# Conditioning weights' blocks begin four panels later in the queue of weight transfers of a flow-matching block

## The chip, the cores and the metric

One core of a Trainium2 chip runs the kernel. The metric is device time in microseconds (us), the median of several executions. Besides these, one execution was profiled; all rows shown here come from it, and their times count from the start of its span.

## What is computed

One layer of a hybrid backbone, float32 throughout: 256 latent tokens and 256 context tokens of width 1024.

```python
sh1, sc1, g1, sh2, sc2, g2 = split(silu(c) @ w_ada + b_ada, 6)     # w_ada: 1024 x 6144
z = modulate(layer_norm_plain(x), sh1, sc1) @ w_in + b_in          # w_in: 1024 x 5904
# p -> pooling mixer, (q, k, v, gates, o) -> mLSTM, (u, v) -> spatial gating, mg -> merge gates
y = (sig(mg_p)*(pool @ w_bp) + sig(mg_m)*(mlstm @ w_bm) + sig(mg_s)*(sgu @ w_bs)) @ w_out
x = layer_norm(alpha*x + g1*y, ln1_g, ln1_b)
h = modulate(layer_norm_plain(x), sh2, sc2)
f = top-4-of-32 clamped SwiGLU experts(h)                          # 12 MB of weights each
out = layer_norm(alpha*x + g2*f, ln2_g, ln2_b)
```

The first third of `w_ada` (`sh1`, `sc1`) is wanted before the input projection. The other two thirds (`g1`, `sh2` and `sc2`, `g2`) are wanted only behind the merge: these are the conditioning weights of the title, 16 blocks of 128 x 2048 floats (1 MB each), called `("ada", 1, k)` and `("ada", 2, k)`, k from 0 to 7.

## The kernel before

**Transfers.** All weights come through one hand-written list, `queue`, issued on SyncE (SP) by `pump` (L149) in list order. A block goes to a free 1 MB slot of the SBUF arena; there are six slots until the merge (an expert's blocks take two slots each). `done(key)` (L174) frees a slot and pumps, so the instruction that last reads a block releases the transfer that comes next in the list; SP works its issues off in order.

**Panels.** `w_in` is cut into 23 blocks `("win", i)` of 256 columns, "panels". A panel is split in two rounded parts so that three matmuls make a float32 product: `split` (L340) casts it on ScalarE (L343), and `low`, run later by `tick`, subtracts on VectorE (L348) and frees its slot. The matmuls of a projection are L251.

**Order of the front part.** The code writes every engine's instructions in one order:

- the first two panels (key columns), then value columns (`v_unit`), each with a piece of convolution (L441, L443) on VectorE;
- a loop over four query units (L991 to L1002); between them steps of `gates` (mLSTM gates; PE L502 to L546, VectorE L510 to L559);
- a loop over 17 `panels` (L1052), each with two units of 24 matmuls. In order: 8, 9, 10, 6, 7, then 11 to 22 (merge gates); below they are "panel loop 0 to 16". Between units, `next(side)` advances a generator `chain` (L957): `state` (VectorE L578, PE L577 and L586, ScalarE L580, L588), `sgu` (PE L743, VectorE L746), `pooling`, `heads` (PE L604 to L628, ScalarE L613, VectorE L615, L633), `head_out`;
- the merge (L1079), the output projection, normalization and routing, and the 32 experts (L1484).

PSUM banks are handed round in small rings: `sps()` has two banks for `gates`, `state`, `sgu` and `heads`.

**Conditioning steps.** `ada_step` (L392) stands at the end of every unit. It takes one conditioning block if that block is the oldest loaded block not yet used: a panel that was loaded before it and is not yet freed blocks it. The first block of each group is scaled on ScalarE (`S.mul`, L398), the seven others are one VectorE instruction over 2048 columns that adds the block before, which is then freed:

```python
V.scalar_tensor_tensor(out=w, in0=w, scalar=sc_[:, k:k + 1], in1=weight(("ada", g, k - 1)), op0=ALU.mult, op1=ALU.add)
done(("ada", g, k - 1))
```

After the last block of a group `ada_reduce` (L407) sums over partitions on TensorE (L417 or L422, L427).

Of the kernel before, what the change touches and what calls it, by code (L numbers as in the profile page):

```python
# [117 lines left out]
def kernel(ctx, tc, x, cx, cols, rows, csts, wsm, wgt, bada, brt, sgub, bdn, bgu,  # L118
# [11 lines left out]
    late = [(("ada", g, k), wada[P * k:P * k + P, 2048 * g:2048 * g + 2048]) for g in (1, 2) for k in range(KB)]  # L130
# [2 lines left out]
    queue.insert(5, (("win", 1), win[1]))  # L133
    for n, i in enumerate([2, 3, 4, 5, 8, 9, 10, 6, 7] + list(range(11, 23))):
        queue.append((("win", i), win[i]))
        if 2 <= n < 18:
            queue.append(late.pop(0))
    queue += [(("br", i), wbr[i]) for i in range(4)]
    queue += [(("out", i), wout[i]) for i in range(4)]
    for e in range(NE):  # L140
# [1548 lines left out]
```

## Time and profile before

| | us |
|---|---|
| median of 3 executions (1279.19 to 1282.16) | 1281.83 |
| the profiled execution, device time | 1278.06 |
| its span | 1276.3 |
| TensorE (PE) busy | 1184.0 (93%) |
| VectorE (DVE) busy | 462.5 (36%) |
| ScalarE (ACT) busy | 285.2 (22%) |

The mean granted clock of TensorE was 0.989. The span holds two very different parts: up to about 320 us the front part, then the experts. So shares of the span say little, and the rows below are of single stretches.

### The profile page before, as it was taken

To read this page: it belongs to the slowest core of one execution; us is meant where nothing else is said; L and a number is where in the kernel's file an instruction comes from. 1 tells how busy PE (TensorE), PEld (TensorE's weight loads), DVE (VectorE), ACT (ScalarE), POOL (GpSimd) and SP (SyncE) were. 2 spreads that over 40 slices of the span, in tenths; PEclk is the share of its full clock that TensorE was granted. 3 is DMA by queue.
4 is the path that set the end of the run, shared out by engine and by line. 5 is a ranking of instruction groups with operands and counts; after the bars stand their busy time and mean duration, and the time that the engine had idled before them with its cause. 6 is when DMAs were issued, how large, how long until landed. Compare 5 with 4: busy or idle time off the path is not lost. (4 is left out here: it accounts for less than half of the span.)

```text
span 1276.3 us, 16505 instructions
## 1 busy us (share of the span) xinstructions
PE 1184.0 (93%) x6619; PEld 609.9 (48%) x6624; DVE 462.5 (36%) x988; ACT 285.2 (22%) x548; POOL 28.4 (2%) x42
## 2 busy tenths in 40 slices
PE   7997999998999999999999999999898998889885
PEld 5897889996333334334433333333333333333321
DVE  6478758796322222222212222222222122222223
ACT  5352655734111111111111111111111111111101
POOL 1000000102000000000000000000000000000000
PEclk9998999998999999999999999999999999999998
DMA  9745657778899999999969999999999999999994
GB/s 390 270 151 215 218 194 284 293 306 322 354 425 426 426 426 427 426 379 428 375 238 386 428 426 427 426 425 427 427 427 426 425 426 427 427 426 425 428 422 179
DMA packets 39758, 471.74 MB, mean 370 GB/s; under 512 B 4561, under 2 KB 4689, under 8 KB 7761
## 3 DMA queue, kind: packets, MB, share of 16 engines
q1 hardware_dynamic: 37440, 464.01, 87.9%
q10 hardware_dynamic: 1552, 4.14, 1.0%
q8 instruction: 89, 1.46, 0.5%
q0 software_dynamic: 640, 1.84, 0.4%
q14 instruction: 37, 0.30, 0.1%
HBM read 468.92 MB, written 1.05 MB: 368 GB/s over the span
## 5 line engine op out<-in xcount | busy, mean ns | idle before, releaser
L1397 PE MATMUL bank<-arena,arena 128*64 128x512 f32 x1808 | 408.9, 596 | 18.1 <-DMA arena<-in_wgu_dram 17.5
L1419 PE MATMUL bank<-arena,arena 128*64 128x512 f32 x1088 | 248.3, 597 | 25.1 <-DMA arena<-in_wdn_dram 17.8
L1397 PEld LDWEIGHTS bank<-arena,arena 128*64 128x64 f32 x1808 | 124.0, 137 | 259.8 <-issue 235.2
L1419 PEld LDWEIGHTS bank<-arena,arena 128*64 128x64 f32 x1088 | 78.6, 136 | 171.9 <-issue 148.9
L251 PE MATMUL bank<-rounded 128*128 128x256 f32 (+1 forms) x1152 | 149.5, 289 | 0.1
L251 PEld LDWEIGHTS bank<-rounded 128*128 128x128 f32 x1152 | 143.9, 195 | 1.8 <-issue 0.6
L1402 DVE TENSOR_SCALAR arena<-bank 128x256 f32<-128x256 f32 x68 | 28.9, 425 | 279.1 <-PE bank L1397 279.1
L1422 DVE SCALAR_TENSOR_TENSOR arena<-bank,arena,g2q 128x512 f32<-128x512 f32 x33 | 24.8, 751 | 266.7 <-PE bank L1419 147.0
L1403 ACT ACTIVATE arena<-arena 128x256 f32<-128x256 f32 x68 | 28.5, 419 | 364.5 <-DVE arena L1402 360.6
L1412 ACT COPY arena<-bank 128x256 f32<-128x256 f32 x68 | 25.4, 373 | 290.5 <-PE bank L1411 290.5
L1397 PE MATMUL bank<-arena 128*64 128x512 f32 x368 | 83.7, 597 | 3.7 <-DMA arena<-in_wgu_dram 3.4
L348 DVE TENSOR_TENSOR rounded<-arena,rounded 128x2048 fp32r<-128x2048 f32 x29 | 66.3, 2285 | 15.1 <-ACT rounded L343 15.1
L1372 PE MATMUL bank<-arena 128*128 128x128 f32 (+1 forms) x576 | 69.9, 275 | 0.0
L1372 PEld LDWEIGHTS bank<-arena 128*128 128x128 f32 x576 | 66.9, 192 | 0.8 <-DVE arena L1404 0.7
L1375 ACT ACTIVATE arena<-bank,shc 128x128 f32<-128x128 f32 (+1 forms) x144 | 53.4, 452 | 51.4 <-PE bank L1372 51.4
L343 ACT CAST rounded<-arena 128x2048 fp32r<-128x2048 f32 x29 | 55.1, 1899 | 11.4 <-PE bank L251 5.6
L1384 DVE TENSOR_SCALAR rounded<-bank 128x256 fp32r<-128x256 f32 x34 | 14.5, 425 | 116.1 <-PE bank L1383 116.1
L1397 PEld LDWEIGHTS bank<-arena 128*64 128x64 f32 x368 | 24.9, 137 | 53.3 <-issue 44.3
L1423 ACT CAST rounded<-arena 128x512 fp32r<-128x512 f32 x33 | 20.4, 619 | 109.4 <-DVE arena L1422 109.4
L1431 PE MATMUL bank<-rounded 64*128 64x512 f32 x264 | 40.7, 418 | 3.6 <-ACT rounded L1423 3.1
L1431 PEld LDWEIGHTS bank<-rounded 64*128 64x128 f32 x264 | 22.8, 184 | 33.9 <-issue 25.1
L1391 PE MATMUL bank<-rounded 128*128 128x512 f32 x68 | 32.4, 476 | 5.8 <-PEq L1508 3.7
(326 smaller groups left out, 890.3 us busy)
## 6 DMA issues: line engine op xcount, KB each, us to landing
arena<-in_wgu_dram SPq DMA_DIRECT2D x127, 2048.0 KB, 29.6
arena<-in_wdn_dram SPq DMA_DIRECT2D x62, 2048.0 KB, 28.0
arena<-in_win_dram SPq DMA_DIRECT2D x23, 1024.0 KB, 5.1
arena<-in_wada_dram SPq DMA_DIRECT2D x16, 1024.0 KB, 5.0
arena<-in_wad_dram SPq DMA_DIRECT2D x8, 1024.0 KB, 10.8
arena<-in_wbr_dram SPq DMA_DIRECT2D x4, 1024.0 KB, 5.6
arena<-in_wout_dram SPq DMA_DIRECT2D x4, 1024.0 KB, 5.6
arena<-in_wdn_dram SPq DMA_DIRECT2D x3, 1024.0 KB, 29.4
```

Source lines behind the costliest of these rows:

```text
L251: mm(o, l, r, start=start and n == 0, stop=stop and n == len(todo) - 1)
L343: S.copy(out=wh[:, 0:2048], in_=w)
L348: V.tensor_tensor(out=wl[:, 0:2048], in0=w, in1=wh[:, 0:2048].bitcast(F32), op=ALU.subtract)
L1372: mm(pg[:, w * k:w * k + w], h2[:, t, 512 * a + P * k:512 * a + P * k + P], b["sl"][:, t].rearrange("p i n -> p (i n)"), start=t == 0, sto ...
L1375: S.activation(out=b["hT"][:, 4 * a + k].rearrange("p i n -> p (i n)"), in_=pg[:, w * k:w * k + w], func=AF.Identity, scale=shc[:, 1, 4 * ...
L1391: mm(pg[:], bse[e % 2][:], bst[:, hf, :], start=True, stop=False, skip_group_check=True)
L1397: mm(pg[64 * q:64 * q + 64, :], hT[:, k, :], wk[:, k % 2, 512 * q:512 * q + 512], start=False, stop=k == KB - 1, skip_group_check=True)
L1402: V.tensor_scalar_min(gc[:], pg[:, 0:256], LIMIT)
L1403: S.activation(out=sg[:], in_=gc[:], func=AF.Sigmoid, scale=SW_ALPHA)
L1412: S.copy(out=b["gT"][:, 4 * hf:4 * hf + 4, :].rearrange("p (q j) n -> p j q n", q=2), in_=pt[:, 0:256].rearrange("p (j q n) -> p j q n", j ...
L1419: mm(py[64 * q:64 * q + 64, :], b["gT"][:, k, :], wk[:, k % 2, 512 * q:512 * q + 512], start=k == 0, stop=k == KB - 1)
L1431: mm(acc[t][hf][:], b["sT"][sl, P * t:P * t + P], y_[sl, :], start=False, stop=last and y_ is ylx, skip_group_check=True)
```

## The change

In the list, the 16 conditioning blocks stood one behind each of the panels number 2 to 17 (n counts panels from panel 2 on). Now the first stands behind n = 6, and n = 7, 9, 11 and 13 have two behind them; the last stands where it stood, behind n = 17. Nothing else is edited; which `ada_step` finds work follows from the list.

```diff
     for n, i in enumerate([2, 3, 4, 5, 8, 9, 10, 6, 7] + list(range(11, 23))):
         queue.append((("win", i), win[i]))
-        if 2 <= n < 18:
+        for _ in range(0 if n < 6 or n > 17 else 2 if n in (7, 9, 11, 13) else 1):
             queue.append(late.pop(0))
+    assert not late
```

## Rows read from the trace of the kernel before

**Rows 1.** Busy time by stretch: span, PE, PEld, DVE, ACT, POOL, granted clock, DMA share, GB/s.
```profile
100.00:125.00 25.00, 18.97 (x136) 17.09 (x137) 22.47 (x42) 4.90 (x8) 0.00 (x0) 0.91 0.56 200
...
150.00:175.00 25.00, 25.00 (x171) 20.95 (x171) 15.87 (x25) 14.87 (x27) 0.00 (x0) 1.00 0.59 210
175.00:200.00 25.00, 24.83 (x194) 22.89 (x190) 16.61 (x21) 13.18 (x25) 0.58 (x1) 1.00 0.62 215
...
325.00:350.00 25.00, 24.54 (x124) 9.73 (x122) 6.65 (x17) 3.71 (x9) 0.00 (x0) 1.00 1.00 415
```

**Rows 2.** Timeline of PE, 60 to 160 us: start, length, instruction, idle before.
```profile
97.02 1.23 PE L520 MATMUL bank<-ident,W 128*8 128x128 f32 x5 [2.37 <-DVE W L514]
97.90 4.19 PE L251 MATMUL bank<-rounded 128*128 128x256 f32 x24
...
116.17 0.44 PE L577 MATMUL bank<-ident,arena 128*128 128x128 f32 x2 [1.69 <-DVE Rc L553]
...
122.63 2.06 PE L586 MATMUL bank<-arena 128*128 128x258 f32 x4 [4.28 <-DVE arena L578]
124.13 4.78 PE L251 MATMUL bank<-rounded 128*128 128x256 f32 x24
...
128.96 1.04 PE L586 MATMUL bank<-arena 128*128 128x258 f32 x4
129.65 3.21 PE L251 MATMUL bank<-rounded 128*128 128x256 f32 x24
```

**Rows 3.** Timeline of DVE, the same stretch.
```profile
93.69 2.35 DVE L400 SCALAR_TENSOR_TENSOR arena<-arena,sc__144 128x2048 f32<-128x2048 f32 x1
95.95 0.48 DVE L455 TENSOR_SCALAR arena<-bank,col 128x256 f32<-128x256 f32 x1
...
98.58 2.35 DVE L400 SCALAR_TENSOR_TENSOR arena<-arena,sc__144 128x2048 f32<-128x2048 f32 x1
...
110.16 2.35 DVE L400 SCALAR_TENSOR_TENSOR arena<-arena,sc__144 128x2048 f32<-128x2048 f32 x1
...
119.14 2.35 DVE L400 SCALAR_TENSOR_TENSOR arena<-arena,sc__144 128x2048 f32<-128x2048 f32 x1
...
122.07 0.75 DVE L578 TENSOR_TENSOR arena<-arena,ee 128x258 f32<-128x258 f32 x2
```

**Rows 4.** Short stretches, columns as in the first group: where the clock was low.
```profile
96.00:100.00 4.00, 2.98 (x15) 2.65 (x16) 3.90 (x11) 0.44 (x2) 0.00 (x0) 0.61 0.92 346
...
124.00:128.00 4.00, 4.00 (x20) 3.85 (x19) 1.01 (x1) 2.17 (x2) 0.00 (x0) 0.55 0.47 197
```

**Rows 5.** Instructions of L400 and of L398: count, ns min/median/max, first and last start.
```profile
L400 DVE SCALAR_TENSOR_TENSOR arena<-arena,sc__144 x14: 2319/2345/2347, 93.7 to 221.8; 128x2048 f32<-128x2048 f32 x14
...
L398 ACT ACTIVATE arena<-arena,sc__144 x2: 2004/2010/2015, 79.7 to 158.8; 128x2048 f32<-128x2048 f32 x2
```

**Rows 6.** Timeline of all engines, 176 to 184 us (panel loop 7).
```profile
177.18 1.90 ACT L343 CAST rounded<-arena 128x2048 fp32r<-128x2048 f32 x1
...
179.12 2.29 DVE L348 TENSOR_TENSOR rounded<-arena,rounded 128x2048 fp32r<-128x2048 f32 x1 [1.36 <-ACT rounded L343]
...
181.32 0.42 DVE L746 TENSOR_TENSOR mx<-bank,arena 128x256 f32<-128x256 f32 x1
...
181.79 0.18 PEld L610 LDWEIGHTS bank<-rounded 40*128 40x128 f32 x1 [0.26 <-DVE mx L746]
```

**Rows 7.** Timeline of ACT from 158 us on.
```profile
205.01 1.90 ACT L343 CAST rounded<-arena 128x2048 fp32r<-128x2048 f32 x1
```

**Rows 8.** Timeline of DVE from 158 us on.
```profile
196.67 0.43 DVE L633 TENSOR_TENSOR arena<-bank,ni 128x258 f32<-128x258 f32 x1 [1.28 <-ACT ni L631]
198.46 2.29 DVE L348 TENSOR_TENSOR rounded<-arena,rounded 128x2048 fp32r<-128x2048 f32 x1 [1.36 <-ACT rounded L343]
```

**Rows 9.** DMA issues of the page: count, KB each, median us to landing.
```profile
arena<-in_win_dram SPq DMA_DIRECT2D x23, 1024.0 KB, 5.1
```

**Rows 10.** What SP waited for, 240 to 330 us: us in total, times, longest.
```profile
SPq L166 <- DVE rounded L348: 31.7, 4, 11.2
SPq L166 <- PEq L1508: 12.2, 1, 12.2
```

## The prediction

> **What bounds the kernel now.** I read the busy time by stretch first, then timelines of the engines where that view shows holes. The reader is to see two regimes. From 325 us on the DMA engines are full: a share of 1.00 and 415 GB/s, with PE at 24.54 of 25 us [rows 1]. That part, the experts, needs a fixed amount of data; it ends earlier only if it starts earlier. Before it, SP's waits are for releases of slots by L348 and the experts' own L1508 [rows 10], not for bandwidth: expert blocks are fetched when the front part sets space free, so what the front part gains, the end should gain.
>
> In the front part PE is full where the panel loop runs (25.00 and 24.83 of 25 us at 150 to 200), but between 100 and 125 us it is busy only 18.97, and there DVE is the full engine, 22.47 [rows 1]. The timeline of PE names the holes: 2.37 us for L514, 1.69 for L553, 4.28 for L578, each a short mixer instruction on DVE [rows 2]. The timeline of DVE shows why these are late: DVE runs almost without a pause, and conditioning steps of 2.35 us stand between its short instructions at 93.69, 98.58, 110.16 and 119.14 [rows 3]. Nothing wants their result before the merge.
>
> **Which steps move.** By the rule of `ada_step` I wrote down, unit by unit, which six blocks are loaded. Before, steps (1,1) to (1,3) fall in the query loop, (1,4) in panel loop 0, one each in 2, 3, 4, the ACT step (2,0) in 5, and one each in 6 to 12; the ACT step (1,0) falls between the value units at 79.7 [rows 5]. After, the list is 2, 3, 4, 5, 8, 9, 10, then (1,0), 6, (1,1), (1,2), 7, (1,3), 11 and so on. Panels now stand in front of the conditioning blocks, so no step finds work until panel 10 is freed: the ACT step (1,0) falls in panel loop 0, (1,1) and (1,2) in loop 2, (1,3) in 3, (1,4) and (1,5) in 4, (1,6) in 5, (1,7) and the ACT step (2,0) in 6, (2,1) in 7, (2,2) and (2,3) in 8. From loop 9 on both lists give the same step in the same unit. So four DVE steps leave 93 to 122 us, and loops 2 to 8 hold ten instead of six. The reduction of group 1 moves from loop 5 to loop 7 with the same matmuls. Bytes, instructions and transfers stay the same in number.
>
> **What leaves.** A step holds DVE for 2.26 us, from its start to that of the next instruction (93.69 to 95.95) [rows 3]. The first hole ends 2.26 us earlier, so 0.1 of 2.37 stays. L553 comes three steps (6.8 us) earlier, and the 1.69 goes. L578 comes four steps, 9.0 us, earlier: its end moves from 122.82 to 113.8. PE, without its holes, is there at 122.63 - 8.34 = 114.3, or about 113.2 with the full clock. The ACT step (1,0) now stands on ACT just ahead of the copy that L586 also needs, 2.0 us [rows 5], which puts that copy at about 114.0: I leave 0.8 of the third hole. Holes: 2.37 + 1.69 + 4.28 - 0.1 - 0.8 = 7.4 us.
>
> **The clock.** Behind the first and the third hole the granted clock is 0.61 and 0.55 over four us, stretches at the half level (1.2 GHz) [rows 4]. There 24 matmuls of L251 take 4.19 and 4.78 us where the same group takes 3.21 later, and L586 takes 2.06 where it later takes 1.04 [rows 2]: 1.0 + 1.6 + 1.0 = 3.6 us. With holes of 0.1 and 0.8 us I expect the clock to stay up and take all of it; the lower bound is nothing.
> The Trainium skill ("TensorE: Matmul & The Clock Gate", Part 1: The HAM clock gate) says that the full clock is held by activity, and that the moment of the change does not hang on the kernel's start, so the same kernel shows differing numbers of slow matmuls from run to run. The trace agrees that low clock follows holes (0.61 and 0.55); that it varies between executions no run here shows. By that rule these 3.6 us would come back only in some executions.
>
> **What arrives.** Loops 2 to 8 get four more DVE steps. DVE is busy 15.87 and 16.61 of 25 us there [rows 1]; over the 75 us of these loops 4 x 2.26 = 9.0 us more is about 3 in 25, which leaves DVE room. What counts is what is queued behind a step. In loops 2 to 5 it is mostly the next panel's L348, whose panel PE wants a loop later, or operands that `heads` wants one or two units later: nothing. One place is tight. In loop 7 the second L610 wants a bank of the two-bank ring that L746 must first empty; it already waits 0.26 us. L746 stands behind L348, and that waited 1.36 us for the cast at 177.18 [rows 6]. The moved ACT step (2,0) now stands directly in front of that cast: cast, L348, L746 and L610 come 2.0 us later. Lower bound zero, if ACT is early there; upper bound 2.0 [rows 5]. I take 2.0, because the chain has no slack in it now.
>
> In loop 8 the second step comes after L633 at 196.67 and ends some 2.4 us later, near 199.5; L348, now at 198.46, moves by 1.0 us [rows 8]. Its result is used in the last third of a unit that starts some 3 us later: nothing. That step also releases panel 18's transfer near 199.5 instead of one unit earlier; with 5.1 us to landing [rows 9] it is there at 204.6, against the cast at 205.01 [rows 7]. Hidden, with 0.4 us to spare; if it lands late, the cast waits, and the panel is used two loops later, so still nothing. All other panels arrive a loop or more ahead.
>
> **Sum.** -7.4 - 3.6 + 2.0 = -9.0 us. Against the profiled execution: 1278.06 - 9.0 = 1269.1. That execution is 3.8 us below the median of the three runs, and a new median will lie as those do: 1281.83 - 9.0 = 1272.8. I predict 1272.5.
>
> **Rivals.** A change under 0.3% (3.8 us) is about what a measurement of this kernel can't tell from none.
>
> *The clock doesn't come back.* The holes close, but PE still falls to half speed near the third hole, where 0.8 us of waiting stays beside short matmuls: -7.4 + 2.0 = -5.4, 1276.4. For it: the low clock lasts beyond the hole itself [rows 4]. Against it: later in the front part holes of some tenths leave it at 1.00 [rows 1].
>
> *The panel loops pay it back.* Steps are now doubled between mixer instructions whose PE partners follow a unit later; if three of the ten come through to PE, 3 x 2.26 = 6.8 goes: -2.2, 1279.6, within the 0.3%. For it: the tight ring in loop 7 [rows 6] shows that the margins of `heads` and `sgu` are short. Against it: ten steps where six cost PE almost nothing now (24.83 to 25.00 busy) [rows 1].
>
> *Hidden anyway.* If the experts' start hung on bandwidth, nothing would move: 1281.8. Against it: SP's waits for releases [rows 10].
>
> *Slower.* One mechanism: DVE's order in loops 2 to 8 becomes the bound, that is, every L348 and mixer instruction queues behind a step and PE waits out each. Ten steps then cost 22.6 us and the ACT step 2.0, against 11.0 gained: +13.6, 1295. It decides for slower once seven or more steps are exposed in full (7 x 2.26 = 15.8 with the ACT step's 2.0, less 11.0 and the 0.3%). For it: DVE is strictly in program order. Against it: a load of about 19 in 25 us, and PE without holes there now.
>
> **How the numbers follow.** Forecast (-6.5 to -12, so 1270 to 1275) 0.56; clock stays low 0.16; paid back 0.16; hidden 0.05; slower 0.07. Faster by over 0.3%: the first two and a little of the third, 0.74; same 0.19; slower 0.07. The range: its low end is the profiled execution less all of the gain without the 2.0, 1278.06 - 11.0 = 1267; its high end takes in the clock's case and most of the paid-back one, 1279.5.
>
> **What would show it.** In the changed profile: no L400 before about 115 us, and the first ten of the DVE steps between there and 200; PE without the three holes and DVE no longer at 22 in 25 at 100 to 125 us; granted clock 1.00 there; the first PE L586 near 114; a new wait of L610 for L746 in loop 7, some 2 us; the experts' first L1397, now at 315, about 9 us earlier, and the end by the same. Wrong would be: holes that stay at the same instructions with another releaser (ACT's copy for L586, the cast of panel 10), new holes at L610, L624 or L714 of the panel loop, or an expert part that starts earlier and ends no earlier.

## The result, and the profile after

The changed kernel took 1273.66 us (median of 7 runs, 1268.46 to 1275.1) against 1280.42 us (7 runs, 1278.16 to 1282.16) for the kernel before, run beside it: a ratio of 0.9941, 95% interval 0.9923 to 0.9959. It is faster by 0.6%. The forecast was 1272.5 us in a range of 1267 to 1279.5, with 0.74 on faster. The profiled execution took 1274.13 us, its span 1272.3 us at a mean granted clock of 0.990; before, these were 1278.06, 1276.3 and 0.989. In the changed kernel all lines from the list of transfers on are one higher: L251 is L252, L400 is L401, L586 is L587, L746 is L747.

First the busy time by stretch, in the columns of [rows 1], of the changed kernel.

```profile
100.00:125.00 25.00, 23.58 (x182) 21.86 (x181) 21.03 (x40) 12.32 (x17) 0.00 (x0) 1.00 0.41 136
125.00:150.00 25.00, 24.66 (x184) 21.01 (x183) 22.14 (x30) 17.51 (x32) 1.76 (x3) 1.00 0.87 301
150.00:175.00 25.00, 22.94 (x158) 19.87 (x157) 16.83 (x23) 13.17 (x25) 0.58 (x1) 0.93 0.62 217
175.00:200.00 25.00, 25.00 (x198) 23.88 (x197) 17.88 (x14) 11.89 (x16) 0.00 (x0) 1.00 0.75 262
```

TensorE went from 18.97 to 23.58 us busy between 100 and 125 us, and the clock from 0.91 to 1.00 [rows 1]. But the stretch from 150 to 175, full before at 25.00 us and 1.00, now stands at 22.94 us and 0.93: something new costs there. VectorE carries at 125 to 150 us what left the stretch before: 22.14 of 25 us, with TensorE at 24.66 beside it. In the kernel before it had 16.64 there:

```profile
125.00:150.00 25.00, 24.58 (x187) 22.69 (x188) 16.64 (x21) 15.68 (x26) 1.77 (x3) 0.95 0.55 199
```

The timeline of TensorE of the changed kernel, where [rows 2] showed the three holes:

```profile
94.82 0.71 PE L521 MATMUL bank<-ident,W 128*8 128x128 f32 x5
95.28 3.12 PE L252 MATMUL bank<-rounded 128*128 128x256 f32 x24
...
110.63 0.38 PE L578 MATMUL bank<-ident,arena 128*128 128x128 f32 x2
...
114.17 1.14 PE L587 MATMUL bank<-arena 128*128 128x258 f32 x4 [1.42 <-ACT arena L581]
114.96 3.23 PE L252 MATMUL bank<-rounded 128*128 128x256 f32 x24
118.02 0.38 PE L578 MATMUL bank<-ident,arena 128*128 128x128 f32 x2
118.25 1.04 PE L587 MATMUL bank<-arena 128*128 128x258 f32 x4
```

L521 and the second L578 follow the work ahead of them without a wait, where L520 had waited 2.37 us and L577 1.69 [rows 2]. L587 still waits 1.42 us in place of 4.28, and for another engine: ScalarE's copy L581. The group of 24 matmuls behind the first hole takes 3.12 us in place of 4.19, that behind the third 3.23 in place of 4.78. The second L587 starts at 118.25, where L586 started at 128.96: 10.7 us earlier.

Then the timelines of ScalarE and VectorE of the changed kernel around that wait:

```profile
111.72 0.24 ACT L561 ACTIVATE ee<-ee 128x48 f32<-128x48 f32 x1
111.87 1.99 ACT L399 ACTIVATE arena<-arena,sc__144 128x2048 f32<-128x2048 f32 x1
113.77 0.62 ACT L581 COPY arena<-bank 128x256 f32<-128x256 f32 x2
```

```profile
113.32 0.75 DVE L579 TENSOR_TENSOR arena<-arena,ee 128x258 f32<-128x258 f32 x2
...
120.50 2.35 DVE L401 SCALAR_TENSOR_TENSOR arena<-arena,sc__144 128x2048 f32<-128x2048 f32 x1
```

The scaling L399 stands directly ahead of L581. The first blending step L401 (one of the DVE conditioning steps) starts at 120.50, behind the products L579 for which the first two L587 wait; four such steps ran before 122 us in [rows 3]. L579 is 8.75 us earlier than L578 was.

Last, panel loop 7 of the changed kernel, in the timelines of ScalarE, VectorE and TensorE. In [rows 6] the second weight load L610 waited 0.26 us here.

```profile
162.96 2.00 ACT L399 ACTIVATE arena<-arena,sc__144 128x2048 f32<-128x2048 f32 x1
164.85 1.89 ACT L344 CAST rounded<-arena 128x2048 fp32r<-128x2048 f32 x1
```

```profile
166.78 2.29 DVE L349 TENSOR_TENSOR rounded<-arena,rounded 128x2048 fp32r<-128x2048 f32 x1 [3.25 <-ACT rounded L344]
168.99 0.42 DVE L747 TENSOR_TENSOR mx<-bank,arena 128x256 f32<-128x256 f32 x1
```

```profile
169.46 0.44 PE L611 MATMUL bank<-rounded 40*128 40x384 f32 x1 [1.90 <-DVE mx L747]
...
170.99 1.23 PE L629 MATMUL bank<-arena 128*128 128x258 f32 x2 [0.16 <-ACT arena L615]
171.66 4.34 PE L252 MATMUL bank<-rounded 128*128 128x256 f32 x24
```

The chain reads from top to bottom: scaling, cast, low part, L747, and TensorE waits 1.90 us. Behind the wait L629 takes 1.23 us and the 24 matmuls 4.34, where such groups take 0.70 and 3.23 at the full clock: 1.6 us more, at a granted clock of 0.73 from 172 to 176 us.

**Where the gain stands along the span.** In the two profiled executions, TensorE is ahead by 10.7 us at the second L587. Loop 7 takes 1.9 in the wait and 1.6 at half clock, of which 0.26 us of waiting was there before. In loop 9 the lead is 7.4 us and stays so until the gathers L1373, matmuls that pick the first experts' tokens once the routing is known. These take 5.44 us in place of 3.81, at a clock of 0.59 from 304 to 308 us. The kernel before has half clock in this stage too (0.50 from 300 to 304 us), but on the eight matmuls L1241, which run while VectorE still works at the routing. First the kernel before, then the changed kernel:

```profile
299.42 6.51 PE L1241 MATMUL bank<-arena,arena 128*128 128x512 f32 x8
...
311.17 3.81 PE L1372 MATMUL bank<-arena 128*128 128x128 f32 x32
```

```profile
291.59 2.82 PE L1242 MATMUL bank<-arena,arena 128*128 128x512 f32 x6
...
303.72 5.44 PE L1373 MATMUL bank<-arena 128*128 128x128 f32 x32
```

From the last router matmuls ahead of them (L1158 at 298.55, L1159 at 291.12) to the first gather it is 12.6 us in both. So half clock on L1241 was hidden behind the routing, and on the gathers it cost 1.6 us. The first expert starts 5.8 us earlier; another stretch at half clock near 540 us takes 1.6; the span ends 4.0 us earlier. Otherwise the 68 starts of L1392, one for each group of the experts, keep the same distances in both executions within 0.4 us, but for one that is 1.5 us late and made up by the next.

### The profile page after: what moved, and what is told of

The parts are those of the page before. It is cut to its first block, busy times and chain, and to the rows that moved or that the text cites. A ratio compares the mean times of both kernels' runs of the same rounds, so it can differ in the third digit from the quotient of the medians.

```text
span 1272.3 us, 16520 instructions
## 1 busy us (share of the span) xinstructions
PE 1183.1 (93%) x6624; PEld 609.3 (48%) x6624; DVE 462.0 (36%) x988; ACT 284.4 (22%) x548; POOL 28.3 (2%) x42
## 5 line engine op out<-in xcount | busy, mean ns | idle before, releaser
L252 PE MATMUL bank<-rounded 128*128 128x256 f32 (+1 forms) x1152 | 148.0, 288 | 0.1
L252 PEld LDWEIGHTS bank<-rounded 128*128 128x128 f32 x1152 | 142.4, 193 | 1.8 <-issue 0.6
L1373 PE MATMUL bank<-arena 128*128 128x128 f32 (+1 forms) x576 | 71.5, 279 | 0.0
L349 DVE TENSOR_TENSOR rounded<-arena,rounded 128x2048 fp32r<-128x2048 f32 x29 | 66.2, 2284 | 10.7 <-ACT rounded L344 10.7
L1373 PEld LDWEIGHTS bank<-arena 128*128 128x128 f32 x576 | 68.5, 196 | 0.8 <-DVE arena L1405 0.7
L1424 ACT CAST rounded<-arena 128x512 fp32r<-128x512 f32 x33 | 20.4, 618 | 109.5 <-DVE arena L1423 109.5
L1432 PE MATMUL bank<-rounded 64*128 64x512 f32 x264 | 41.4, 423 | 3.6 <-ACT rounded L1424 3.1
L1432 PEld LDWEIGHTS bank<-rounded 64*128 64x128 f32 x264 | 23.2, 186 | 33.9 <-issue 25.1
L1392 PE MATMUL bank<-rounded 128*128 128x512 f32 x68 | 32.2, 474 | 5.9 <-PEq L1509 3.6
```

The lines of the kernel that those rows point to most:

```text
L252: mm(o, l, r, start=start and n == 0, stop=stop and n == len(todo) - 1)
L349: V.tensor_tensor(out=wl[:, 0:2048], in0=w, in1=wh[:, 0:2048].bitcast(F32), op=ALU.subtract)
L1373: mm(pg[:, w * k:w * k + w], h2[:, t, 512 * a + P * k:512 * a + P * k + P], b["sl"][:, t].rearrange("p i n -> p (i n)"), start=t == 0, sto ...
L1392: mm(pg[:], bse[e % 2][:], bst[:, hf, :], start=True, stop=False, skip_group_check=True)
L1432: mm(acc[t][hf][:], b["sT"][sl, P * t:P * t + P], y_[sl, :], start=False, stop=last and y_ is ylx, skip_group_check=True)
```

## The experiments

Each ratio is to the kernel before, run beside it on the same chip. Shifts within a span are counted from one mark, the first matmul of the gates, since the ten profiled executions reach it between 86.90 and 90.12 us. It stands here for the kernel before and the changed kernel:

```profile
88.63 0.28 PE L502 MATMUL bank<-lf,tri 128*128 128x8 f32 x2
```

```profile
88.69 0.28 PE L503 MATMUL bank<-lf,tri 128*128 128x8 f32 x2
```

**The changed kernel again** (`again`, no edit).

> The changed kernel, not edited. Both theories expect 1273.7 us within its own spread (1268.5 to 1275.1). What differs is the profile. If the half-clock stretches behind 300 us hang on chance (where the clock's change falls among the matmuls), the waits of PE up to 300 us come back within 0.1 us (0.1, none, 1.4 us in place of the three holes, 1.9 us at L611 in panel loop 7), but the stretch that cost 1.6 us at the first gathers, or the one at 538 to 544 us, is somewhere else or missing. If these belong to the change, both stand where they stood.

Measured: 1271.44 us (6 runs), ratio 0.9948 (0.993 to 0.9967); the profiled execution 1270.58 us. Its waits are those of the first profile: none at L521, 1.42 us at the first L587, 1.90 in loop 7. What differs is the clock. TensorE's timeline of this execution in loop 7:

```profile
169.25 0.44 PE L611 MATMUL bank<-rounded 40*128 40x384 f32 x1 [1.90 <-DVE mx L747]
...
170.77 0.70 PE L629 MATMUL bank<-arena 128*128 128x258 f32 x2 [0.15 <-ACT arena L615]
171.12 3.24 PE L252 MATMUL bank<-rounded 128*128 128x256 f32 x24
```

And the windows from 172 to 176 us and 540 to 544 us, of the changed kernel's first profile and of this one:

```profile
172.00:176.00 4.00, 4.00 (x27) 3.99 (x26) 2.69 (x2) 0.63 (x2) 0.00 (x0) 0.73 0.30 123
...
540.00:544.00 4.00, 4.00 (x15) 1.27 (x13) 0.00 (x0) 0.00 (x0) 0.00 (x0) 0.65 1.01 424
```

```profile
172.00:176.00 4.00, 4.00 (x30) 3.63 (x29) 2.69 (x2) 1.11 (x4) 0.00 (x0) 1.00 0.38 119
...
540.00:544.00 4.00, 4.00 (x27) 2.39 (x24) 0.00 (x0) 0.37 (x1) 0.00 (x0) 1.00 0.99 387
```

The same wait in the same program is followed by half clock in one execution and not in the other. Of the five profiles here that have this wait of 1.90 us, three show half clock behind it (the changed kernel's first, `old_places` and `early_one`: 4.34, 4.73 and 4.56 us for the 24 matmuls) and two don't (this one and `two_steps`: 3.24 and 3.23). The wait belongs to the change; the 1.6 us behind it, and those near 540 us, belong to an execution. The gathers, though, were slow in this execution too:

```profile
302.32 5.06 PE L1373 MATMUL bank<-arena 128*128 128x128 f32 x32
```

In this execution the lead over the kernel before is 9.05 us in loop 9 and 7.6 at the first expert.

**The old places, without the old list** (`old_places`). The changed list stays; four instructions of L401's form, which change no value, stand where the four early steps stood.

```
+        def old_place(key):
+            w = weight(key)
+            V.scalar_tensor_tensor(out=w, in0=w, scalar=1.0, in1=w, op0=ALU.mult, op1=ALU.max)
...
                 ada_step()
+                if (i, b) != (1, 1):
+                    old_place(("win", 10))
...
+                if (n, ui) == (0, 0):
+                    old_place(("win", 6))
```

> The changed list, with four extra DVE instructions of the same form and size as a conditioning step where the four steps stood before (three in the query loop, one in loop 0); they rewrite a panel block with its own values. If DVE's order makes the holes, the three come back (2.4, 1.7, 4.3 us) with the same instructions behind them and the half clock with them, and the wait in loop 7 comes on top: slower than the kernel before by about 3 us, ratio 1.002 to 1.003. If the earlier arrival of the panels is what helps, the time stays near that of the change, 1273 to 1275.

Measured: 1281.14 us (10 runs), ratio 1.001 (0.9996 to 1.0024): the gain is gone. TensorE's timeline of it, with lines four higher than in the changed kernel:

```profile
96.99 0.71 PE L525 MATMUL bank<-ident,W 128*8 128x128 f32 x5 [2.32 <-DVE W L519]
...
116.03 0.44 PE L582 MATMUL bank<-ident,arena 128*128 128x128 f32 x2 [2.79 <-DVE Rc L558]
...
122.43 2.06 PE L591 MATMUL bank<-arena 128*128 128x258 f32 x4 [3.02 <-DVE arena L583]
```

All three holes are back, 8.13 us in sum against 8.34, for the same instructions of VectorE, with L591 at half clock; behind the first hole the clock stayed full (L525 takes 0.71 us, where L520 took 1.23). The wait of loop 7 is there as well (1.90 us, L615 for L751). The median is less above the kernel before than the 1.002 to 1.003 expected, but the interval reaches 1.0024. SyncE issues the panels up to the first hole as in the changed kernel, the last two of them at 60.30 and 82.18 us against 60.33 and 82.22. So the changed list by itself closes nothing: it is VectorE's order that opens and closes the holes.

**Half of the change** (`two_steps`). The blocks begin two panels later in place of four, so that two of the four early steps stay.

```
-            if 2 <= n < 18:
+            for _ in range(0 if n < 4 or n > 17 else 2 if n in (11, 13) else 1):
```

> The kernel before with the blocks two panels later in the list in place of four, and the two doubles behind the 11th and 13th entries (with the count of the entries from 0). Of the four blending steps that stood on VectorE ahead of the state in the kernel before, two remain (at the second query panel and in panel loop 0). Theory (each early blending step holds VectorE for 2.35 us, and the holes shrink in whole steps): the first hole (2.37 us) goes, the third stays at 2 us or more with the half clock behind it; the state's first L587 comes 3 to 5 us earlier than before, not 8; the wait in panel loop 7 (1.90 us and up to 1.6 of half clock) is paid in full, so that the end gains 0 to 2 us: 1277 to 1281, ratio 0.997 to 1.000. Rival (what counts is how early the panels land): the holes close as in the changed kernel in proportion to the panels brought forward, half of the gain, all three a bit, ratio 0.997. Rival (the last early step alone makes the holes): all three stay, ratio 1.000 or above.

Measured: 1276.51 us (10 runs), ratio 0.9973 (0.996 to 0.9987): at the fast edge of the first theory, and as the first rival has it too. TensorE's timeline decides:

```profile
109.92 0.44 PE L578 MATMUL bank<-ident,arena 128*128 128x128 f32 x2 [0.92 <-DVE Rc L554]
110.41 1.69 PE L483 MATMUL bank<-zb,identb 128*128 128x512 bf16 x7
116.38 2.06 PE L587 MATMUL bank<-arena 128*128 128x258 f32 x4 [4.28 <-DVE arena L579]
```

The first hole is gone, the second 0.92 us, the third 4.28 as before, with half clock behind it. Counted from the mark (86.90 here), L587 is 29.48 us away, against 34.00 before and 25.48 after: 4.52 us for two steps, 8.52 for four, that is 2.26 us for each of the two, as VectorE's slot in [rows 3], and less for the four because ScalarE ends the third hole then.

**Filling the holes** (`filled_holes`). The kernel before, with TensorE kept busy in the holes by matmuls whose result nothing reads (9 more, 10 and 16 more).

```
+            idle7(9)
...
+                if h == 1:
+                    idle7(10)
...
-                    idle7(8)
+                    idle7(24)
```

> The kernel before, with more idle matmuls into a spare bank where the three holes are (9, 10 and 16 more), so that PE works through most of them and DVE's order is left as it was. If the holes are timed by DVE, L520, the second L577 and L586 start where they started; the clock stays up and only what lies behind the third hole is won: 1.0 at L586 and 1.6 at the next L251, 2.6 us in all, ratio 0.998. If the clock's share is worth its whole 3.6 us by itself: 0.997. If the clock doesn't come back from idle matmuls, or the gain of the change has nothing to do with it: 1.000.

Measured: 1277.47 us (12 runs), ratio 0.9991 (0.9974 to 1.0007). The median is 2.9 us below that of the kernel before, as the first theory has it, but the interval holds 1, so the times alone don't tell it from no change. The profile tells more:

```profile
120.97 1.11 PE L589 MATMUL bank<-arena 128*128 128x258 f32 x4 [0.80 <-DVE arena L581]
121.73 3.21 PE L251 MATMUL bank<-rounded 128*128 128x256 f32 x24
```

L589 is 34.00 us from the mark (86.97 here), as L586 was before: VectorE sets it, whatever TensorE does meanwhile. Behind it the clock is full: 1.11 and 3.21 us in place of 2.06 and 4.78. In this execution the 2.5 us of low clock behind the third hole are gone, with TensorE working through most of it. Loop 9 starts 2.3 us earlier than before, counted from the mark; two stretches of half clock near 541 and 654 us, which the kernel before did not have, take 3.3 us again.

**The scaling one loop later, by the list** (`scale_later`). The doubles stand behind the entries 7, 9, 13 and 15, so that the scaling of (2,0) falls into loop 7, behind its cast.

```
-        for _ in range(0 if n < 6 or n > 17 else 2 if n in (7, 9, 11, 13) else 1):
+        for _ in range(0 if n < 6 or n > 17 else 2 if n in (7, 9, 13, 15) else 1):
```

> The changed kernel with the doubled panels 7, 9, 13, 15 in place of 7, 9, 11, 13: the scaling step on ACT, (2,0), falls in loop 7 behind the cast instead of in loop 6 in front of it. If the wait of L611 for L747 is the ACT step's 2.0 us and the half clock behind it is its consequence, both go: PE reaches the end of loop 8 some 3.4 us earlier, the time is about 1270.3. If the doubled DVE steps are what fills loop 7, the wait stays at 1.9 us and the time at 1273.7.

Measured: 1274.61 us (8 runs), ratio 0.9967 (0.9954 to 0.9981): not faster than the changed kernel. The wait in loop 7 is gone, as expected, and loop 9 starts 96.19 us from the mark (99.52 in the changed kernel's first profile, 98.10 in `again`). But the doubles behind later entries hold later panels up. ScalarE's casts wait 5.7 us for a panel between 195 and 207 us (2.2 in `again`), a blending step (200.74) gets ahead of the panel's low part on VectorE, and TensorE stands still where it never did:

```profile
205.31 4.99 PE L252 MATMUL bank<-rounded 128*128 128x256 f32 x27 [2.54 <-DVE rounded L349]
```

With the clock at 0.83 from 205 to 215 us, TensorE takes 4.6 us more than in `again` between the start of loop 9 and the router matmuls near 291 us. The wait of loop 7 is worth closing, but not by moving transfers.

**The scaling of (2,0) one unit earlier, in the code** (`early_two`). Transfers and steps stay as changed; only this ScalarE instruction is issued where ScalarE is idle, and `ada_step` then leaves it out.

```
+        def ada_scale(g):
...
+            S.mul(out=w, in_=w, mul=sc_[:, 0:1])
...
                 ada_step()
+                if (n, ui) == (6, 0):
+                    ada_scale(2)
```

> The changed kernel with one edit: the scaling of block (2,0) on ScalarE (L399, 2.00 us) is issued one unit earlier, at the end of the first unit of panel loop 6, where ScalarE waits 2.23 us for TensorE, and no longer stands ahead of the panel copy (L344) of loop 7. The list of transfers, and every other instruction, keep their order. Theory (the scaling ahead of the copy is the whole cause of the new wait in loop 7): TensorE's wait of 1.90 us for L747 falls to under 0.4, the half clock that one of two executions showed behind it cannot occur, and the start of panel loop 9 comes 1.9 us earlier counted from the start of the second transposes of the state; 1.9 to 2.7 us below the changed kernel beside it, 1268 to 1270, ratio to the kernel before 0.9930. Rival (the copy was late for its weights, or VectorE's own queue is late): the wait stays at 1.5 or more. Rival (a place in loop 6 is as tight): a new wait of up to 1.9 us appears there, for ScalarE L1035, and the time is that of the changed kernel, ratio 0.9945.

Measured: 1270.44 us (6 runs), ratio 0.992 (0.9898 to 0.9942). In its timelines the scaling runs at 156.53, the cast of loop 7 starts at 161.28 right behind L641, and TensorE no longer waits (L620 there is L611 of the changed kernel):

```profile
165.18 0.44 PE L620 MATMUL bank<-rounded 40*128 40x384 f32 x1
165.54 0.34 PE L621 MATMUL bank<-maskw,identb 128*128 128x384 bf16 x1
165.89 0.44 PE L620 MATMUL bank<-rounded 40*128 40x384 f32 x1
```

Loop 9 starts 96.22 us from the mark, against 98.10 in `again` and 99.52 in the first profile of the changed kernel, and no new wait shows in loop 6. The first theory holds: the scaling ahead of the cast is the whole of that wait (1.88 of 1.90 us against `again`). The medians of `again` and of this kernel, 1271.44 and 1270.44 us, are from different chips and too near to tell 2 us; the timelines tell it.

**The scaling of (1,0) earlier** (`early_one`): the same edit, by `ada_scale(1)` behind the second query unit.

> The changed kernel with the scaling of block (1,0) on ScalarE (L399, 1.99 us) issued some 14 us earlier, into the idle time of 8.96 us that ScalarE has between 97 and 106 us, so that it no longer stands ahead of the state's copy L581. Theory (two late engines behind each other): L581 starts near 111.7 in place of 113.55, but the first L587 also needs VectorE's L579, whose first pair ends near 113.86; the wait of 1.42 us falls by 0.1 to 0.4 only and is now put down to VectorE, and the time is that of the changed kernel (1270 to 1274, ratio 0.9945). Rival (the scaling is the only cause of that wait): the wait goes from 1.42 to under 0.2 and the time falls by 1.3 us, ratio 0.9935.

Measured: 1270.04 us (4 runs), ratio 0.9914 (0.9893 to 0.9936). The wait is still there, with another name (L596 and L588 are L587 and L579 of the changed kernel):

```profile
115.32 1.11 PE L596 MATMUL bank<-arena 128*128 128x258 f32 x4 [1.12 <-DVE arena L588]
```

1.12 us for VectorE in place of 1.42 for ScalarE: two engines were late together, and taking one away gave 0.3 us. The interval leaves out the first theory's 0.9945 and holds the rival's 0.9935. But the trace speaks against the rival, and the changed kernel itself was not run on this chip, so that the times, four runs from 1268.2 to 1274.3 us, don't tell the two apart.

**Both, and the low part of panel 10 put off** (`early_both_low`). The two scalings are issued as in the two runs above; the rest of the edit:

```
-            ahead(order[0][1] == panels[n + 1][0] if n + 1 < len(panels) else order[0] == ("br", 0))
+            if n != 1:
+                ahead(order[0][1] == panels[n + 1][0] if n + 1 < len(panels) else order[0] == ("br", 0))
...
-                tick()
-                if ui == 0 and order[0] != ("br", 1):
+                if n:
+                    tick()
+                if ui == 0 and n > 1 and order[0] != ("br", 1):
```

> The changed kernel with both scalings early, and the low part of panel 10 (L349, 2.29 us of VectorE at 110.23) put off by one panel loop, so that it stands behind the state's first products L579. Theory (with both late engines relieved the third hole closes): the first L587 follows the eight matmuls L483 ahead of it with under 0.4 us of wait, near 112.6; the wait in panel loop 7 is gone; panel loop 9 starts 3.0 to 3.4 us earlier than in the changed kernel, counted from the same early mark; 1267 to 1269, ratio to the kernel before 0.9920. Rival (the low part is now late for its own products in panel loop 2): TensorE waits 1 to 2 us for L349 near 114 to 116, and only the 1.9 us of loop 7 are kept, ratio 0.9930. Rival (later stages take it back, the transfers of the experts' weights set the end): the waits go but the end comes no earlier than in the changed kernel.

Measured: 1267.3 us (5 runs, 1265.11 to 1268.69), ratio 0.9895 (0.9876 to 0.9914): faster than both kernels. In the timeline of TensorE the third hole is closed:

```profile
111.00 1.69 PE L492 MATMUL bank<-zb,identb 128*128 128x512 bf16 x7
112.52 1.10 PE L596 MATMUL bank<-arena 128*128 128x258 f32 x4
113.27 3.22 PE L252 MATMUL bank<-rounded 128*128 128x256 f32 x24
```

and VectorE's timeline has the state's products ahead of the low part:

```profile
111.94 0.77 DVE L588 TENSOR_TENSOR arena<-arena,ee 128x258 f32<-128x258 f32 x2 [1.32 <-ACT ee L570]
112.62 2.29 DVE L349 TENSOR_TENSOR rounded<-arena,rounded 128x2048 fp32r<-128x2048 f32 x1
```

No wait for L349 appears near 114 us. Loop 9 starts 94.58 us from the mark, 3.5 us before `again`, where 3.0 to 3.4 were expected; the ratio is below the expected 0.9920 as well. The busy time from 100 to 125 us shows why a share of busy time could not have told this:

```profile
100.00:125.00 25.00, 24.95 (x192) 23.39 (x192) 22.66 (x41) 11.38 (x17) 0.00 (x0) 1.00 0.46 164
```

VectorE is as busy as in the kernel before (22.66 us against 22.47), and TensorE is full (24.95 against 18.97). What held TensorE up was VectorE's order, not its load.

## Why the prediction was right, point by point

**Steps.** Where each step falls came out as written down: no L401 before 115 us, the scaling of (1,0) just ahead of the state's copy, that of (2,0) ahead of the cast of loop 7, and the second step of loop 8 (189.66) as the last that stands elsewhere.

**Holes, -7.4 forecast.** 2.37 + 1.69 + 4.28 - 1.42 = 6.9 us measured. The first hole closed whole (0.1 had been left). The third kept 1.42 in place of 0.8: L587 started when the copy let it, at 114.17 against 114.0 forecast, but TensorE was there at 112.75, some 0.45 us before the 113.2 forecast. That VectorE's products were nearly as late as the copy was not seen; `early_one` and `early_both_low` show it.

**Clock, -3.6.** The lead at the second L587, 10.8 us from the mark, less 6.9 for holes is about 3.8. Two sizes in the term were off and nearly cancel, by the starts of the groups: L520, at half clock too, was not counted (0.4), and L586 gave 0.7 in place of 1.0. The clock came back in all six profiles of a kernel without the four early steps (1.00 from 100 to 125 us in the two of the changed kernel, `scale_later`, `early_two`, `early_one` and `early_both_low`), and was low with the holes in `old_places` (0.84 there) and `two_steps` (0.86). The rival that it would not come back falls for this place.

**New wait in loop 7, +2.0.** 1.90 us, by the chain named. `early_two` removes it with the scaling alone.

**Panel loops pay it back, slower.** Both fall: TensorE has 24.66 of 25 us at 125 to 150 and 25.00 at 175 to 200 us, so of the steps that arrived none but the scaling reached it. `scale_later` shows how near that rival was: with two doubles moved a few panels on, a step did cost TensorE 2.54 us.

**Hidden anyway.** It falls: the first expert starts earlier, and its groups keep their distances to the end.

**A bound of the rival "slower".** It was mis-added: not seven but six exposed steps would have done, 6 x 2.26 + 2.0 - 11.0 = 4.6 us, above the 3.8.

**A weak sign.** "DVE no longer at 22 in 25" came true by little, 21.03 us against 22.47, and `early_both_low` shows 22.66 without a hole. The sign does not tell the mechanism from its rivals.

**What was missed.** "The experts' first L1397 about 9 us earlier, and the end by the same": it was 5.8 and 4.0 us in the first profile, about 7.5 for both in `again`. The mechanism stands and a size was off. The sum counted half clock only where it goes away. It can also come behind a new wait (1.6 us in loop 7), and it can lie elsewhere within a stage that had it before: on the gathers (1.6 us, and 1.25 in `again`) in place of the matmuls L1241. The 1.6 us near 540 us came behind a wait of 1.56 us (L1432 for ScalarE's L1424) that the kernel before has too, without half clock behind it. Between the medians beside each other 6.8 us was gained, and 9.0 in `again`, against the forecast of 9.0. That the time itself came within 1.2 us of the forecast is in part luck: the sum started from 1281.83 us, and the kernel before took 1280.42 beside the changed one, so the gain was 2.2 us short and the start 1.4 too high.

The Trainium skill ("TensorE: Matmul & The Clock Gate", Part 1: The HAM clock gate) says that the number of slow matmuls of one kernel differs from run to run; here loop 7 ran at 0.73 in one execution of the changed kernel and at 1.00 in another. By that rule the 3.6 us forecast at the holes would have come back in some executions only, and the six profiles above all had the full clock there.

**Still open.** What makes the clock fall behind a given short wait in one execution and not in the next: no run here controls it. The same group of the experts lost its 1.6 us (the one near 540 us in the changed kernel) in five of the ten profiles: the changed kernel's first, `early_two`, `early_both_low`, `filled_holes` and `old_places`, whose experts start anywhere between 302 and 320 us; it did not in the kernel before (314.74), in `again` (307.13) or in the other three. The gathers took 4.65 to 5.44 us in seven of the ten, with the old order of steps (`old_places`) as with the new, and 3.81 in the kernel before, `filled_holes` and `early_both_low`; in these three the half clock lay on the eight matmuls L1241 (L1244 and L1257 there). Whether the changed list makes the first more likely is not shown: the kernel before was profiled once.

## What to carry to other kernels

On an engine that runs in program order, work that nobody wants yet costs what stands behind it: look for long instructions between short ones on which TensorE waits, and price the move by the slot, here 2.26 us for each. Before moving them, follow the whole order to where they land, the single step on another engine too; at both places that kept part of the gain here a scaling of 2.0 us on ScalarE stood in the way, and issuing it into ScalarE's idle time cost nothing that the traces show. Where a wait has two late engines behind it, the profile names one, and relieving that one gives only the difference.

## What the runs showed of the hardware

Runs of one kernel spread with the mean granted clock. Of 42 runs of the kernel before, the eleven at 0.990 or 0.991 took 1277.9 us in the median (1275.5 to 1280.7), and the eleven at 0.981 to 0.984 took 1282.1 (1281.3 to 1283.9). Where TensorE had no other wait to hide it in, a stretch at half clock cost 1.6 us in loop 7, at the gathers and near 540 us of the changed kernel's first profile, and 1.25 at the gathers of `again`; on L1241 it was hidden. One more or less in an execution is about a fifth of what the change gave. So a single profile of the changed kernel showed the gain at 4.0 us, and another at 7.5; the single steps within a trace, from a common mark, told more: 1.90 us of wait removed came out as 1.88.
